# A gated MLP's up projection as seven block products per pair of column blocks, with the hidden values and the residual kept in DRAM and the down projection as a stage of its own

## The chip, the cores and the metric

The kernel runs on one core of one Trainium2 chip. The metric is the device time of one execution in microseconds (us); before the change the median of three runs is 1703.65 us (1700.2 to 1703.98). A core has TensorE (PE; matmuls, and PEld for its weight loads), VectorE (DVE), ScalarE (ACT), GpSimd (POOL) and SyncE (SP). SP issues nearly all DMAs of this kernel, each engine works through its own list in order, and the DMAs themselves run on 16 DMA engines. SBUF is the on-chip memory, PSUM the banks that matmuls write to, DRAM the memory outside the core.

## The reference, cut to what matters

One layer: RMSNorm, an input projection, an attention branch and a state space branch, a gated sum of the two, `w_out` and a residual add, then the channel mixer, which is where the change lies, and a last RMSNorm:

```
xn   = rmsnorm(x, norm2_g)                     # x: 1024 prompt tokens and 8 x 4 sample tokens, 1024 wide
up   = xn @ w_up                               # 1024 x 5632: a value half and a gate half of 2816 columns
val, gate = up[:, :2816], up[:, 2816:]
act  = silu(causal depthwise conv of width 3 over positions of val, + conv_b)
x    = x + (act * gate) @ w_down               # 2816 x 1024
y    = rmsnorm(x, norm_f_g)
```

The last two positions of `val` are outputs too. Everything is float32.

## The kernel before, in words

The 1056 tokens lie along the free axis: four blocks of 264 columns (`C`), each with 256 prompt tokens (every fourth position) and 8 sample tokens, so channels lie on the 128 partitions. A float32 matrix is held as a high and a low part (`split`, L184: an ACT cast, then a DVE subtraction), and a product of two such matrices is three matmuls: low weight by high data, high by low, high by high.

`load_w` (L147 to L157) brings a weight block in by SP (L154), casts its high part on ACT (L155) and subtracts for the low part on DVE (L156), from a pool of two buffers. `gemm` (its matmuls are L174) multiplies 8 blocks of 128 contraction rows in chunks of 352 columns: 8 x 3 x 3 = 72 matmuls for 128 output channels.

The order around the change is this. The merge stage (L1317 to L1330) loads the gated branches back from DRAM (`ck`, 24 loads of 176 KB by SP at L1324, and as many by ACT) and forms the pairs `mh`, `ml`. The `w_out` stage (L1336 to L1355) makes eight blocks `y` = product + residual (`xcol`), which stay in SBUF, their sums of squares on ACT and POOL (L1353, L1354), and the eight pairs `X`. Then, at L1370 to L1381, ones matmuls and transposes give the factors of the norm, `rb2`.

The MLP works on 22 blocks of 128 hidden channels. `up(f)` multiplies the value block, scales it by `rb2` (DVE, L1391), shifts it by one position for the convolution (POOL, L1392 to L1394), forms the convolution (ACT L1396, DVE L1397 and L1398), the silu (ACT L1399) and a product with `rb2` (POOL L1400), then multiplies the gate block and splits the result into `hh`, `hl`. `down` (L1414 to L1419) multiplies a group of three such blocks (the last two groups have two) by `w_down` and adds into `y`; a group's `down` follows the next group's `up`. The last group's `down` is fused with the last norm and the outputs (L1444 to L1510). The convolution states are turned and sent out at L1429 to L1438.

The program is written in this order, and a scheduler orders each engine's list by its own priorities within it; buffers of pools make the waits.

## Time and profile before

| | |
|---|---|
| median of three runs (lowest to highest) | 1703.65 us (1700.2 to 1703.98) |
| the profiled execution's own time; its span | 1697.35 us; 1695.4 us |
| PE, DVE, ACT, POOL busy in the span | 1623.4, 791.0, 490.8, 434.9 us |
| mean granted TensorE clock | 0.984 of full speed |
| DMA over the span | 158.62 MB, 94 GB/s |

The span runs from the first to the last instruction; the profiled execution's time is 1.95 us longer. Each view of the profile counts in us from the span's start. Matmuls are pipelined, so the time that a matmul costs is the distance between the starts of two neighbours and not the duration shown for one.

### The profile page before, as it was taken

To read this page: it belongs to the slowest core of one execution; us is meant where nothing else is said; L and a number is where in the kernel's file an instruction comes from. 1 tells how busy PE (TensorE), PEld (TensorE's weight loads), DVE (VectorE), ACT (ScalarE), POOL (GpSimd) and SP (SyncE) were. 2 spreads that over 40 slices of the span, in tenths; PEclk is the share of its full clock that TensorE was granted. 3 is DMA by queue.
4 is the path that set the end of the run, shared out by engine and by line. 5 is a ranking of instruction groups with operands and counts; after the bars stand their busy time and mean duration, and the time that the engine had idled before them with its cause. 6 is when DMAs were issued, how large, how long until landed. Compare 5 with 4: busy or idle time off the path is not lost.

```text
span 1695.4 us, 25830 instructions
## 1 busy us (share of the span) xinstructions
PE 1623.4 (96%) x10431; PEld 1547.1 (91%) x10431; DVE 791.0 (47%) x1437; ACT 490.8 (29%) x941; POOL 434.9 (26%) x483
## 2 busy tenths in 40 slices
PE   5999978999999989999999999999999999999997
PEld 5898877998888878888999999999999999999996
DVE  5545989233443534235533443434344443444455
ACT  5211221234443433326423222121211212121226
POOL 0669374012122322313322211010111102010115
PEclk9999999999999999999999999999999999999999
DMA  8263311355346445686311110201102021021122
GB/s 228 66 178 120 107 59 51 99 144 134 93 108 149 127 113 195 221 278 189 105 51 38 51 43 24 72 27 50 54 24 72 27 62 43 29 60 33 57 61 103
DMA packets 225010, 158.62 MB, mean 94 GB/s; under 512 B 31173, under 2 KB 210863, under 8 KB 224890
## 3 DMA queue, kind: packets, MB, share of 16 engines
q1 hardware_dynamic: 211210, 135.05, 27.2%
q0 software_dynamic: 3328, 11.54, 2.0%
q10 hardware_dynamic: 10352, 10.38, 1.9%
q8 instruction: 82, 1.34, 0.3%
q14 instruction: 38, 0.31, 0.1%
HBM read 128.97 MB, written 29.92 MB: 94 GB/s over the span
## 4 chain that ended last, share of the span: by engine, by line
PE 55%; DMA 2%; ACT 1%; DVE 1%; POOL 1%; issue 1%; DVEq 0%; ACTq 0%; POOLq 0%; SPq 0%
PE pg L174 53%; DMA msd<-go 1%; PE pa L144 1%; DMA ck<-sgd 1%; DMA go<-sgd 0%; DMA cache<-in_cache_kv_w_dram 0%; PE pD L1225 0%; PE pg L1489 0%; ACT go L1493 0%; PE pg L144 0%; DVE hh L1506 0%; PE pe L144 0%; DVE ml L186 0%; ACT xl L1297 0%; PE pD L1228 0%
## 5 line engine op out<-in xcount | busy, mean ns | idle before, releaser
L174 PE MATMUL pg<-xh,wlo 128*128 128x352 f32 x1872 | 484.2, 332 | 3.0 <-ACT pt__5401 L870 1.5
L174 PE MATMUL pg<-xh,whi 128*128 128x352 f32 x1872 | 470.5, 325 | 0.0
L174 PE MATMUL pg<-xl,whi 128*128 128x352 f32 x1872 | 468.5, 324 | 0.0
L174 PEld LDWEIGHTS pg<-xh,wlo 128*128 128x128 f32 x1872 | 329.5, 189 | 14.5 <-issue 5.6
L174 PEld LDWEIGHTS pg<-xh,whi 128*128 128x128 f32 x1872 | 332.2, 189 | 0.0
L174 PEld LDWEIGHTS pg<-xl,whi 128*128 128x128 f32 x1872 | 331.7, 189 | 0.3
L155 ACT CAST whi<-wraw 128x1024 fp32r<-128x1024 f32 (+2 forms) x154 | 130.9, 850 | 581.4 <-PE pg L174 393.0
L156 DVE TENSOR_TENSOR wlo<-wraw,whi 128x1024 fp32r<-128x1024 f32 (+2 forms) x154 | 162.2, 1053 | 99.5 <-ACT whi L155 96.7
L1392 POOL COPY ext<-ext 128x510 f32<-128x510 f32 x22 | 15.6, 710 | 522.2 <-DVE ext L1391 522.2
L174 PE MATMUL pg<-hh,wlo 128*128 128x352 f32 x480 | 148.0, 325 | 0.0
L174 PE MATMUL pg<-hl,whi 128*128 128x352 f32 x480 | 147.0, 322 | 0.0
L174 PE MATMUL pg<-hh,whi 128*128 128x352 f32 x480 | 146.5, 323 | 0.0
L1419 DVE TENSOR_TENSOR y<-pg,y 128x352 f32<-128x352 f32 x168 | 84.5, 524 | 98.9 <-PE pg L174 98.2
L962 POOL TENSOR_TENSOR qb<-kt,qb 128x512 f32<-128x512 f32 x48 | 64.8, 1364 | 246.3 <-DMA qb<-qd 150.1
L1391 DVE TENSOR_TENSOR ext<-pg,rb 128x352 f32<-128x352 f32 x66 | 32.7, 524 | 154.2 <-PE pg L174 154.2
L174 PEld LDWEIGHTS pg<-hh,wlo 128*128 128x128 f32 x480 | 88.9, 188 | 0.5
L174 PEld LDWEIGHTS pg<-hl,whi 128*128 128x128 f32 x480 | 89.1, 188 | 0.0
L174 PEld LDWEIGHTS pg<-hh,whi 128*128 128x128 f32 x480 | 88.7, 188 | 0.0
L1406 DVE TENSOR_TENSOR go<-pg,cv 128x352 f32<-128x352 f32 x66 | 31.2, 520 | 111.7 <-PE pg L174 111.7
L1400 POOL TENSOR_TENSOR cv<-cv,rb 128x1056 f32<-128x1056 f32 x22 | 54.2, 2463 | 55.0 <-ACT cv L1399 52.7
L1007 ACT COPY pTs<-pT 128x256 f32<-128x256 f32 (+1 forms) x48 | 22.5, 469 | 123.5 <-PE pT L144 121.5
L174 PE MATMUL pg<-yh,wlo 128*128 128x352 f32 x144 | 48.2, 345 | 4.1 <-ACT go L471 3.4
(643 smaller groups left out, 2338.4 us busy)
## 6 DMA issues: line engine op xcount, KB each, us to landing
wraw<-in_w_up_dram SPq DMA_DIRECT2D x44, 512.0 KB
wraw<-in_w_in_dram SPq DMA_DIRECT2D x38, 512.0 KB
qb<-qd SPq DMA_DIRECT2D x48, 256.0 KB
wraw<-in_w_down_dram SPq DMA_DIRECT2D x48, 192.0 KB
sgd<-go SPq DMA_DIRECT2D x16, 528.0 KB
kt<-in_cache_kv_w_dram SPq DMA_DIRECT2D x32, 256.0 KB
cache<-in_cache_kv_w_dram POOLq DMA_DIRECT2D x16, 512.0 KB, 6.5
go<-sgd SPq DMA_DIRECT2D x8, 528.0 KB
```

The costliest lines, as they stand in the source:

```text
L144: PE.transpose(out, in_, ident[:n, :n])
L155: A_.copy(hi, raw)
L156: E2.tensor_tensor(lo, raw, hi.bitcast(F32), OP.subtract)
L174: PE.matmul(ps[c][:, :CH], wt[:, k0 + k, m0:m0 + P], xt[:, c * CH:(c + 1) * CH], start=k == 0 and j == 0, stop=k == n - 1 and j == 2)
L962: G_.tensor_tensor(qb, kv_, qb, OP.mult)
L1007: A_.copy(pTs[:, :2 * n * P], pT[:, :2 * n * P])
L1391: V_.tensor_tensor(ef[:, 2 * C + c * CH:2 * C + (c + 1) * CH], ps[c][:, :CH], rb2[:, cs(c)], OP.mult)
L1392: G_.tensor_copy(e[:, 0:2, 1:256], e[:, 4:6, 0:255])
L1400: G_.tensor_tensor(cv, cv, rb2, OP.mult)
L1406: V_.tensor_tensor(t[:, cs(c)], ps[c][:, :CH], cv[:, cs(c)], OP.mult)
L1419: V_.tensor_tensor(y[m][:, cs(c)], ps[c][:, :CH], y[m][:, cs(c)], OP.add)
```

## The change

`w_up` is used in another way. For each of the 22 hidden blocks the value block V and the gate block G are taken together as one matrix of two block columns, the contraction is cut into two halves of 512 rows, and the tokens into two halves of 528 columns. Seven block products (each 4 x 3 x 2 = 24 matmuls of 264 columns) take the place of eight. The data side needs sums of blocks: `operands` makes seven pairs out of each pair of channel blocks (j, j + 4) with four subtractions and seven splits. The weight side needs four sums and five more splits for each block, and the results are put together by seven additions.

What this moves besides: the residual `xcol` goes to DRAM (`xtd`) and comes back block by block; `y` goes to DRAM (`yd2`), is scaled by the norm's weights in place and is not kept; the gated hidden block goes to DRAM (`hd`). When all 22 blocks are done, `w_down` runs as a stage over four token quarters of 264 columns: each quarter loads its hidden values again, splits them into the places of the operands, loads all of `w_down` (so four times in all), and sends its rows out.

The diff, cut to its core:

```diff
+        xtd = dr.tile([D, T], F32, name="xtd")
+        for k in range(KD):
+            nc.sync.dma_start(xtd[k * P:(k + 1) * P], xcol[k])
...
+        def operands(k, pl, a, b):
+            tA, tB = (yt_.tile([P, T], F32, name="tt", bufs=2) for _ in range(2))
+            V_.tensor_tensor(tA[:, H1], a[:, H2], a[:, H1], OP.subtract)
+            V_.tensor_tensor(tA[:, H2], b[:, H2], tA[:, H1], OP.subtract)
+            V_.tensor_tensor(tB[:, H1], b[:, H2], a[:, H2], OP.subtract)
+            V_.tensor_tensor(tB[:, H2], b[:, H1], tA[:, H2], OP.subtract)
+            XO[k] = {}
+            for o, src in enumerate((a[:, H1], b[:, H1], b[:, H2], tA[:, H1], tA[:, H2], tB[:, H1], tB[:, H2])):
+                hi, lo = (pl.tile([P, HALF], F32R, name=f"x{k}{o}{x}") for x in "hl")
+                split(hi, lo, src)
+                XO[k][o] = (hi, lo)
+        kept = []
+        for j in range(NK):
+            ys = []
+            for m in (j, j + NK):
+                w = load_w(I['w_out'][0][:, m * P:(m + 1) * P], KD, pw=wb)
+                ps = gbanks()
+                gemm(ps, w, list(zip(mh, ml)))
+                y = yt_.tile([P, T], F32, name="yt", bufs=3)
+                nc.sync.dma_start(y, xtd[m * P:(m + 1) * P])
+                for c in range(NCH):
+                    V_.tensor_tensor(y[:, cs(c)], ps[c][:, :CH], y[:, cs(c)], OP.add)
+                nc.sync.dma_start(yd2[m * P:(m + 1) * P], y)
+                if m == 0:
+                    A_.activation(sqa, y, AF.Square)
+                else:
+                    t = yt_.tile([P, T], F32, name="tt", bufs=2)
+                    A_.activation(t, y, AF.Square)
+                    G_.tensor_tensor(sqa, sqa, t, OP.add)
+                A_.activation(y, y, AF.Copy, scale=g2c[:, m:m + 1])
+                ys.append(y)
+            if j < NK - 1:
+                operands(j, xa, *ys)
...
+        operands(NK - 1, xb, *ys)
...
+        def product(w, o):
+            ps = pu_.tile([P, 2, 512], F32, name="pu")
+            for k in range(NK):
+                runs = [(c, j) for j in range(3) for c in range(2)]
+                if k in (0, NK - 1):
+                    runs.sort()
+                for c, j in runs:
+                    wt, xt = ((1, 0), (0, 1), (0, 0))[j]
+                    PE.matmul(ps[:, c, :C], w[wt][:, k], XO[k][o][xt][:, c * C:(c + 1) * C],
+                              start=k == 0 and j == 0, stop=k == NK - 1 and j == 2)
+            return ps[:, :, :C]
...
+            raw = []
+            for c0 in (f * P, DFF + f * P):
+                r = wb.tile([P, KD, P], F32, name="wraw")
+                nc.sync.dma_start(r, I['w_up'][0][:, c0:c0 + P].rearrange("(k p) m -> p k m", p=P))
+                raw.append(r)
+            v, g = raw
+            hi = wb.tile([P, KD, P], F32R, name="whi")
+            lo = wb.tile([P, KD, P], F32R, name="wlo")
+            split(hi, lo, v)
+            A11, A12 = ((hi[:, x:x + NK], lo[:, x:x + NK]) for x in (0, NK))
+            S1, S2, S3, S4_ = (sr.tile([P, NK, P], F32, name=f"S{x}") for x in range(4))
+            V_.tensor_tensor(S1, g[:, :NK], g[:, NK:], OP.add)
+            V_.tensor_tensor(S2, S1, v[:, :NK], OP.subtract)
+            V_.tensor_tensor(S3, v[:, :NK], g[:, :NK], OP.subtract)
+            V_.tensor_tensor(S4_, v[:, NK:], S2, OP.subtract)
+            def parts(src):
+                hi, lo = (sr.tile([P, NK, P], F32R, name=f"s{x}", bufs=6) for x in "hl")
+                split(hi, lo, src)
+                return hi, lo
...
+            s2_, s1_, s3_, s4_, a22 = (parts(t) for t in (S2, S1, S3, S4_, g[:, NK:]))
+            r1, u2, u3, u4 = (h2(ff.tile([P, HALF], F32, name=n)) for n in ("r1", "u2", "u3", "u4"))
+            gt = ff.tile([P, T], F32, name="gt", bufs=2)
+            A_.copy(r1, product(A11, 0))
+            V_.tensor_tensor(u2, product(s2_, 4), r1, OP.add)
+            V_.tensor_tensor(e[:, 2:4], product(A12, 1), r1, OP.add)
+            V_.tensor_tensor(e[:, 2:4], e[:, 2:4], h2(rb2[:, H1]), OP.mult)
+            V_.tensor_tensor(u4, product(s1_, 3), u2, OP.add)
+            m7 = product(s3_, 5)
+            V_.tensor_tensor(h2(gt[:, H2]), m7, u4, OP.add)
+            V_.tensor_tensor(u3, m7, u2, OP.add)
+            V_.tensor_tensor(e[:, 4:6], product(s4_, 2), u4, OP.add)
+            V_.tensor_tensor(e[:, 4:6], e[:, 4:6], h2(rb2[:, H2]), OP.mult)
+            V_.tensor_tensor(h2(gt[:, H1]), product(a22, 6), u3, OP.add)
...
+            V_.tensor_tensor(gt, gt, cv, OP.mult)
+            nc.sync.dma_start(hd[f * P:(f + 1) * P], gt)
+        for f in range(NF):
+            up(f)
...
+            co_ = ff.tile([P, T], F32, name="gt", bufs=2)[:18, :512]
...
+        def hidden(q):
+            out = []
+            for j in range(NH):
+                k, o = places[q % 2 * NH + j]
+                pl = xa if k < NK - 1 else xb
+                hi, lo = (pl.tile([P, HALF], F32R, name=f"x{k}{o}{x}") for x in "hl")
+                r = wb.tile([P, KD, P], F32, name="wraw").rearrange("p k m -> p (k m)")[:, :HALF]
+                nc.sync.dma_start(h2(r), hd[2 * j * P:(2 * j + 2) * P, q * C:(q + 1) * C].rearrange("(f p) c -> p f c", p=P))
+                split(hi, lo, r)
+                out += [(hi[:, x * C:(x + 1) * C], lo[:, x * C:(x + 1) * C]) for x in range(2)]
+            return out
...
+            yo = wb.tile([P, KD, P], F32, name="wlo").rearrange("p k m -> p (k m)")[:rows]
+            A_.activation(yo, yT, AF.Square, accum_out=f[:, 0:1])
+            rsqrt(f[:, 1:2], f[:, 0:1], f[:, 2:3], V_)
+            V_.scalar_tensor_tensor(yo, yT, f[:, 1:2], gf[:rows], OP.mult, OP.mult)
+            nc.sync.dma_start(dst, yo)
...
+        hs_ = hidden(0)
+        for q in range(S4):
+            y = fb.tile([P, KD, C], F32, name="y")
+            nc.sync.dma_start(y, yd2[:, q * C:(q + 1) * C].rearrange("(m p) c -> p m c", p=P))
+            nxt = None
+            yT = [wb.tile([P, KD, P], F32, name="whi").rearrange("p k m -> p (k m)") for _ in range(2)]
+            for m in range(0, KD, 2):
+                ps = [pg.tile([P, 512], F32, name="pd") for _ in range(2)]
+                for k0 in range(0, NF, 4):
+                    n = min(4, NF - k0)
+                    w = load_w(I['w_down'][0][k0 * P:(k0 + n) * P, m * P:(m + 2) * P], n, mw=2 * P, pw=w2,
+                               bufs=({"bufs": 4}, {}))
+                    for x in range(2):
+                        for k in range(n):
+                            xh, xl = hs_[k0 + k]
+                            for j, (wt, xt) in enumerate(((w[1], xh), (w[0], xl), (w[0], xh))):
+                                PE.matmul(ps[x][:, :C], wt[:, k, x * P:(x + 1) * P], xt,
+                                          start=k0 + k == 0 and j == 0, stop=k0 + k == NF - 1 and j == 2)
+                for x in range(2):
+                    V_.tensor_tensor(y[:, m + x], ps[x][:, :C], y[:, m + x], OP.add)
+                if m == 0 and q + 1 < S4:
+                    nxt = hidden(q + 1)
+                if m % 4 == 2:
+                    for b in range(2):
+                        turned_half(yT[b], m // 4, P, lambda k, b=b: y[:, k, b * P:(b + 1) * P])
+            for b in range(2):
+                norm_out(2 * q + b, yT[b], P, ypv[q, b])
+            G_.tensor_copy(sy.rearrange("p k (b s) -> p k b s", s=S4)[:, :, :, q], y[:, :, 256:])
+            hs_ = nxt
```

On SyncE, around the loads for `w_out` (`ck` are the gated branches, `go<-sgd` their first part, `wraw<-in_w_out_dram` a weight block, `xtd<-` a block of the residual on its way to DRAM), before:

```order
L1273 DMA go<-sgd 128x1056 x2
L154 DMA wraw<-in_w_out_dram 128x8x128
L1273 DMA go<-sgd 128x1056
L1281 DMA go<-in_x_sample_dram 32x1024
L1324 DMA ck<-sgd 128x352 x6
L154 DMA wraw<-in_w_out_dram 128x8x128
L1324 DMA ck<-sgd 128x352 x8
L154 DMA wraw<-in_w_out_dram 128x8x128
L1324 DMA ck<-sgd 128x352 x9
L154 DMA wraw<-in_w_out_dram 128x8x128
L1324 DMA ck<-sgd 128x352
L154 DMA wraw<-in_w_out_dram 128x8x128 x4
```

and now:

```order
L1275 DMA go<-sgd 128x1056 x3
L1328 DMA ck<-sgd 128x352 x6
L1283 DMA go<-in_x_sample_dram 32x1024
L1302 DMA xtd<-xl_7610 128x1056 x2
L1302 DMA xtd<-xl_7611 128x1056 x2
L1302 DMA xtd<-xl_7612 128x1056 x2
L1302 DMA xtd<-xl_7613 128x1056 x2
L1328 DMA ck<-sgd 128x352 x18
L156 DMA wraw<-in_w_out_dram 128x8x128
L1372 DMA yt<-xtd 128x1056
L156 DMA wraw<-in_w_out_dram 128x8x128
L1372 DMA yt<-xtd 128x1056 x2
```

The first load for `w_out` stood ahead of all 24 `ck` loads and the next three between them; now it stands behind all 24, and eight writes to `xtd` stand ahead of the last 18.

On SyncE, where the last output of the up projection meets the first weights of the down projection (`out_dram<-` are the convolution states), before:

```order
L1437 DMA out_dram<-go 1x512
L154 DMA wraw<-in_w_down_dram 128x2x128
L1438 DMA out_dram<-go 8x512
L1437 DMA out_dram<-go 1x512
L1438 DMA out_dram<-go 8x512
L1437 DMA out_dram<-go 1x512
L154 DMA wraw<-in_w_down_dram 128x2x128
L1438 DMA out_dram<-go 8x512
L1437 DMA out_dram<-go 1x512
L1438 DMA out_dram<-go 8x512
L1437 DMA out_dram<-go 1x256
```

and now (with what each row waits for, `Activation` being ACT and `DMAHW` an earlier DMA):

```order
L1485 DMA hd<-gt 128x1056 [waits DMAHW4_49,DVE_49]
L1499 DMA out_dram<-gt 8x512 [waits DMAHW5_49]
L1519 DMA wraw<-hd 128x2x264 [waits DMAHW6_49,DMAHW4_49]
L1519 DMA wraw<-hd 128x2x264 [waits DMAHW7_49]
L1498 DMA out_dram<-gt 1x512 [waits DMAHW0_49,Activation_49]
L1499 DMA out_dram<-gt 8x512 [waits DMAHW1_49]
L1498 DMA out_dram<-gt 1x512 [waits DMAHW2_49]
L1499 DMA out_dram<-gt 8x512 [waits DMAHW3_49]
```

and, behind six more of the small outputs:

```order
L1498 DMA out_dram<-gt 1x256 [waits DMAHW2_49]
L1499 DMA out_dram<-gt 8x256 [waits DMAHW3_49]
L1519 DMA wraw<-hd 128x2x264 [waits DMAHW4_49,DVE_49]
L1519 DMA wraw<-hd 128x2x264 [waits DMAHW5_49,DVE_49]
L1547 DMA y<-yd_8218 128x8x264 [waits DMAHW6_49,PE_49]
L156 DMA wraw<-in_w_down_dram 128x4x256 [waits DMAHW0_49,DMAHW1_49,DMASW7_49,DMAHW2_49,DMASW4_49,DMAHW3_49,DMASW3_49,DMAHW7_49,DMASW0_49,Pool_49]
L156 DMA wraw<-in_w_down_dram 128x4x256 [waits DMASW5_49,DMASW1_49]
```

The 24 small outputs lay among weight loads whose products went on. Now all of them stand ahead of the first load of `w_down`, the last twelve behind two loads that wait for the last hidden block's way to DRAM.

On VectorE, one hidden block in the middle of the up projection, before (the block's value half, its gate half and its split; `pg` is PSUM):

```order
L1391 TENSOR_TENSOR ext_8977<-pg,rb_7772 128x352 x3
L156 TENSOR_TENSOR wlo<-wraw,whi 128x1024
L1397 SCALAR_TENSOR_TENSOR cv<-ext_8977,cw,cv 128x1056
L1398 SCALAR_TENSOR_TENSOR cv<-ext_8977,cw,cv 128x1056
L1406 TENSOR_TENSOR go<-pg,cv 128x352 x3
L156 TENSOR_TENSOR wlo<-wraw,whi 128x1024
L186 TENSOR_TENSOR hl<-go,hh 128x1056
```

and now the first half of a block (`S` are sums of weight blocks, `sl` and `wlo` low parts, `pu` PSUM):

```order
L1450 TENSOR_TENSOR S_10569<-wraw 128x512
L1452 TENSOR_TENSOR S_10571<-wraw 128x512
L1451 TENSOR_TENSOR S_10570<-S_10569,wraw 128x512
L1480 SCALAR_TENSOR_TENSOR cv<-ext_9136,cw,cv 128x1056
L1453 TENSOR_TENSOR S_10572<-wraw,S_10570 128x512
L188 TENSOR_TENSOR sl<-S_10570,sh 128x512
L1481 SCALAR_TENSOR_TENSOR cv<-ext_9136,cw,cv 128x1056
L1464 TENSOR_TENSOR u_10361<-pu,r_10360 128x528
L188 TENSOR_TENSOR sl<-S_10569,sh 128x512
L1465 TENSOR_TENSOR ext_9136<-pu,r_10360 128x528
L1466 TENSOR_TENSOR ext_9136<-ext_9136,rb_8208 128x528
L188 TENSOR_TENSOR wlo<-wraw,whi 128x1024
```

The list of a block grew from 11 to 22 instructions, and the first sum of the next block's weights opens it.

## Rows read from the trace of the kernel before

**Rows 1.** The page: engine, busy us, share of the span, instructions.

```profile
PE 1623.4 (96%) x10431; PEld 1547.1 (91%) x10431; DVE 791.0 (47%) x1437; ACT 490.8 (29%) x941; POOL 434.9 (26%) x483
```

**Rows 2.** The chain that ended last, in order of time: start us, us, what.

```profile
761.84 3.94 DMA msd<-go
...
765.91 2.35 DMA go<-in_x_sample_dram
...
807.87 105.01 PE pg L174 x640
...
1265.74 365.68 PE pg L174 x2268
...
1652.59 3.49 PE pg L144 x32
```

**Rows 3.** Timeline of TensorE: start us, us, engine, line, operation; starts are read.

```profile
59.72 0.29 PE L311 MATMUL pg<-xl,uwh 128*128 128x264 f32 x1
...
66.06 0.28 PE L311 MATMUL pg<-xh,uwh 128*128 128x264 f32 x1
...
809.18 0.50 PE L174 MATMUL pg<-ah,whi 128*128 128x352 f32 x1
...
811.23 0.50 PE L174 MATMUL pg<-mh,wlo 128*128 128x352 f32 x1
...
904.32 0.32 PE L174 MATMUL pg<-xh,wlo 128*128 128x352 f32 x1
```

**Rows 4.** Timeline of SyncE, issue of the loads before w_out.

```profile
801.34 0.38 SPq L154 DMA_DIRECT2D wraw<-in_w_out_dram  x1
801.82 12.13 SPq L1324 DMA_DIRECT2D ck<-sgd  x9
...
816.00 0.53 SPq L1324 DMA_DIRECT2D ck<-sgd  x1
```

**Rows 5.** Groups of ScalarE after 900 us: busy us, mean ns, idle before.

```profile
L155 ACT CAST whi<-wraw 128x1024 fp32r<-128x1024 f32 x45 | 47.4, 1054 | 271.2 <-PE pg L174 195.4 <-issue 75.8
L1396 ACT ACTIVATE cv<-ext,cw 128x1056 f32<-128x1056 f32 x22 | 28.0, 1271 | 15.3 <-POOL ext L1392 15.3
...
L1399 ACT ACTIVATE cv<-cv 128x1056 f32<-128x1056 f32 x22 | 23.9, 1087 | 59.3 <-DVE cv L1398 59.3
```

**Rows 6.** Groups of VectorE after 900 us.

```profile
L156 DVE TENSOR_TENSOR wlo<-wraw,whi 128x1024 fp32r<-128x1024 f32 x45 | 55.3, 1229 | 31.3 <-ACT whi L155 31.3
L1391 DVE TENSOR_TENSOR ext<-pg,rb 128x352 f32<-128x352 f32 x66 | 32.7, 524 | 154.2 <-PE pg L174 154.2
...
L1398 DVE SCALAR_TENSOR_TENSOR cv<-ext,cw,cv 128x1056 f32<-128x1056 f32 x22 | 29.3, 1334 | 0.8
...
L156 DVE TENSOR_TENSOR wlo<-wraw,whi 128x384 fp32r<-128x384 f32 x48 | 26.8, 558 | 1.8
...
L1381 DVE COPY rb<-pe 128x512 f32<-128x512 f32 x2 | 1.3, 685 | 0.2 <-PE pe L144 0.2
```

**Rows 7.** Windows: us, busy us and count by engine, clock, DMA share, GB/s.

```profile
660.00:680.00 20.00, 16.60 (x112) 15.71 (x111) 9.64 (x16) 8.81 (x12) 2.02 (x3) 0.91 1.00 368
780.00:790.00 10.00, 9.66 (x61) 8.71 (x60) 3.42 (x7) 5.10 (x15) 3.48 (x4) 0.95 0.20 52
790.00:800.00 10.00, 10.00 (x64) 10.00 (x63) 8.07 (x14) 6.14 (x14) 8.18 (x8) 1.00 0.85 255
```

**Rows 8.** Groups of GpSimd after 900 us.

```profile
L1400 POOL TENSOR_TENSOR cv<-cv,rb 128x1056 f32<-128x1056 f32 x22 | 54.2, 2463 | 55.0 <-ACT cv L1399 52.7 <-issue 2.4
...
L1392 POOL COPY ext<-ext 128x510 f32<-128x510 f32 x22 | 15.6, 710 | 522.2 <-DVE ext L1391 522.2
```

**Rows 9.** Timeline of VectorE and GpSimd, one hidden block.

```profile
1327.91 1.23 DVE L156 TENSOR_TENSOR wlo<-wraw,whi 128x1024 fp32r<-128x1024 f32 x1 [0.60 <-ACT whi L155]
...
1327.99 1.20 POOL L1394 COPY cso<-ext 128x18 f32<-128x18 f32 x1
```

**Rows 10.** Line 1394 on GpSimd, 900 to 1650 us: ns min/median/max, first and last start.

```profile
L1394 POOL COPY cso<-ext x22: 192/1198/1212, 924.1 to 1618.3; 128x18 f32<-128x18 f32 x22
```

188 lines of the change are left out of this document (55 added, 133 removed).

## Prediction

> **What bounds the kernel now.** I read the page first: TensorE is busy 1623.4 of 1695.4 us and VectorE less than half of them [rows 1]. The chain of waits says the same from the other side. From 807.87 us it is one stretch of matmuls after another, the longest 2268 matmuls of 352 columns in 365.68 us, or 0.1612 us each [rows 2]; in the MLP nothing but TensorE sets the time. So the profile pays for fewer matmul columns at that rate, and charges for every wait that gets between two matmuls. The first matmul of the MLP starts at 904.32 us [rows 3], and 791.1 us are left to the end of the span. All sums below set the new length of this part, and what happens ahead of it, against these 791.1 us. They are made against the profiled execution (span 1695.4, own time 1697.35 us), which is 0.4% under the median of the runs, 1703.65; I move the difference over to the median unchanged.
>
> **Matmuls.** Out go 22 x 2 x 72 = 3168 matmuls of the up projection (510.8 us at 0.1612), 1440 of the down projection (232.2 us) and the last group's wide ones. In come 22 x 7 x 24 = 3696 matmuls and 4 x 8 x 22 x 3 = 2112, all of 264 columns. That width is in the trace, with the weights changed at every matmul as here: 52 steps lie between the starts at 59.72 and 66.06 us, 0.1219 us each [rows 3]. The up projection then costs 450.5 us and the down projection 257.5 us. The saving is one product of eight in the up projection alone, and a little of it goes to the narrower matmul: three quarters of 0.1612 would be 0.1209, and at that value the two stages would cost 5.8 us less. I keep 0.1219.
>
> **The start of w_out: 10.5 us later.** Its first weight load stood ahead of the 24 branch loads and was long there. Now it is issued behind the last of them. That one goes out at 816.00 to 816.53 now, and two weight loads with their waits stood ahead of it; without these I take 812.5. The weight load then needs its issue (0.38 [rows 4]), its way (a 528 KB transfer took 3.94 us, a small one 2.35 [rows 2]; I take 3), the ACT cast of 1.05 [rows 5] and the low part, 1.23 [rows 6]: 818.2. Ahead of the last 18 branch loads SP now writes 4.3 MB to DRAM. At 368 GB/s, the most that the trace shows, that is 12 us of all DMA engines, and they are free for 80% of the time from 780 to 790 us and for 15% in the next 10 [rows 7]; I take 2 us of delay, with 0 and 12 as ends. So w_out starts at 820 instead of 811.23 [rows 3], 9 us later, and from idle: between 809.18 and 811.23 a matmul took 0.293 us (7 steps) [rows 3], the pace of the lower clock of 1.2 GHz, which lasted some 12 matmuls after a wait and so costs 1.6 us.
>
> **From w_out into the up projection: 7 us.** Before, the first value block and the gate's weights were ready and the ones matmuls alone waited. Now the last operands are made after the last product. ACT may scale the last y in place only when its copy to DRAM has landed (evacuation 0.5, issue 0.4, way 3, scaling 1.2: about 5 us after w_out's end), and the casts of the weight sums stand behind that scaling on ACT. The first product (2.9 us) needs nothing of it; the second begins about 7 us after the end of w_out, and a later one waits about 1 us for VectorE. I count 5 us of waits and 2 us for the small matmuls that were there before too.
>
> **The up projection: 452.5 us, with 2 us of stalls.** Per block TensorE works 7 x 24 x 0.1219 = 20.5 us. What VectorE must do in that time I price by interpolating: 352 columns from PSUM 0.524 and 512 from PSUM 0.685, so 0.70 for 528; 384 columns in SBUF 0.558 and 1024 in 1.229, so 0.69 for 512 and 0.71 for 528 [rows 6]. Seven additions from PSUM are 4.9, four sums 2.8, five low parts 3.5, the value's low part 1.23, two scalings 1.4, two convolution steps 2.7, the last product 1.25: 17.8 us. To that comes a wait: only two raw buffers exist, so the gate block of the next f is loaded after the last low part of this one is taken, and its first sum stands behind it on VectorE. From that low part to the next one along VectorE's list: load 3.4, then 16.4 us of instructions (17.8 less the two that run in the load's shadow), in all 19.8 us against 20.5. So TensorE stays the bound, by 0.7 us per block. The three PSUM buffers cover single delays of about 3 us. ACT (1.05, five half casts, 1.27, 1.09 and a copy: under 7 us [rows 5]) and POOL (2.46, 0.71 and two tiny copies: under 4 [rows 8]) are far from it. The 2 us of stalls are for the first block; A below has the upper end.
>
> **From up to down: 29 us.** This is the largest charge. Nothing of w_down can be loaded before SP has passed what stands ahead of it. After the last product: the last value rows are scaled, POOL shifts them (0.71 [rows 8]), ACT forms the convolution (1.27) behind one of the six small copies, VectorE adds twice (2.7), ACT takes the silu (1.09 [rows 5]), POOL multiplies (2.46 [rows 8]), VectorE multiplies (1.25); with the handovers the hidden block is issued to DRAM 10 us after the last product and lands at 12.7. SP holds the next reload for that, then issues 12 small outputs, whose copies wait for a shared buffer, two more reloads and 1.1 MB of y, each up to 0.38 us of issue; the first w_down load goes out at about 19.6, lands behind that y at 24.5, and with cast and low part the first matmul runs at 27.4 us. The clock falls in such a wait; 1.6 us as above. As ends I take 18 us (the small outputs find their buffers free) and 38 us (each group of outputs waits its full 3.94 us).
>
> **The down projection: 267.5 us.** Matmuls 257.5; 64 transposes of 0.109 (32 in 3.49 us [rows 2]) are 7.0; stalls 3. Per quarter 64.4 us of matmuls need 11.5 MB of weights, 3.0 of hidden values, 1.1 of y and 1.0 of output: 16.6 MB, 258 GB/s. The trace shows 368 with all DMA engines busy [rows 7], so this fits with a third to spare. The 3 us of stalls are for the first loads of a quarter; the upper end is B.
>
> **The end: 15 us** after the last matmul: an addition and the turns, 1; four copies of half a cast and three squares of a cast on ACT [rows 5], 5.3; two scalings of 1.3 (as L1398 [rows 6]) and a third for the sample rows, 3.9; the factors of the norm between them, 1.5; issue and transfer, 3 (2.35 to 3.94 [rows 2]). The ends are 13 and 19.
>
> Sum: 10.6 + 7 + 452.5 + 29 + 267.5 + 15 = 781.6, against 791.1: 9.5 us less. I round to 9 and forecast **1694.6 us**.
>
> **Rivals.**
> *A. VectorE becomes the bound in the up projection, and the kernel gets slower.* POOL and VectorE hinder one another. At 1327.99 POOL's tiny copy took 1.20 us, ending as VectorE's subtraction from 1327.91 ends [rows 9]; alone it takes 0.19, and half of the 22 take about 1.2 [rows 10]. The other direction matters now: POOL's product of 2.46 us stands beside the scaling and the low parts of the next block, and an instruction that comes 1 us into it and waits for its end loses 1.5 us. A decides from 20.5 - 19.8 = 0.7 us per block. With 1 us lost a block costs 0.3 more, with 2 lost 1.3 more: 7 to 29 us over 22 blocks. I put it at 1.5 lost, 18 us, 1712. The rule for this is in the Trainium skill, "SBUF — State Buffer", Who interferes with whom: VectorE with two SBUF inputs and a GpSimd instruction that reads SBUF exclude each other for whole instructions, and the one that issues later waits. The trace's copy agrees with it (0.19 against 1.20 us), and by it A happens in every block in which the two meet. Against it: the seven additions take only one of their inputs from SBUF, and POOL's product need not fall on a two-input instruction in every block.
> *B. The down stage is bound by its loads.* SP's list mixes weight loads with reloads that wait for two raw buffers, and one wait holds all behind it. If it gets 220 GB/s on average instead of 258, the 66 MB take 300 us and the time is 1735. For it: SP alone issues everything. Against it: three pairs and four raw blocks of weights, each worth 2.9 us of matmuls, are ahead.
> *C. The two transitions cost half.* The outputs' buffers come free earlier, the first weights come at 18 us, and w_out starts only 5 us late: 15 us less, 1680. For it: nearly all of these transfers are small, and 2.35 us is the row for a small one. Against it: w_down's first load stands behind the way of the last hidden block in any case, 12.7 us.
> *D. The transitions cost more.* One of them at its upper end (38 us at the second instead of 27.4) or half of it at both: about 10 more, 1705, no change. For it: each wait there follows the last, so none hides behind another. Against: the ends take every transfer at the slowest row.
>
> **How the numbers follow.** Forecast as above, 1686 to 1702: 0.42. A 0.16, B 0.11, C 0.15, D 0.16. What a measurement of this kernel can tell from no change is about 0.3%, 5 us. Faster by more (below 1698.5): 0.37 of the main case and all of C, 0.52. Within: the other 0.05, 0.13 of D, 0.03 of A, 0.21. Slower: 0.13 of A, all of B, 0.03 of D, 0.27. The range that leaves out two cases in ten runs from 1679 to 1720; it leaves out most of B and the lower half of C.
>
> **What would show it.** Right: 0.122 us per matmul in both stages; TensorE unbroken in the up stage at about 20.5 us per block; a gap of 25 to 30 us before the first matmul of the down stage, ended by the first weights; w_out about 9 us later. Wrong: blocks of more than 21 us with TensorE waiting for VectorE (A); many waits for w_down's casts (B); a gap of under 20 us (C).

## The result

The changed kernel takes 1713.65 us (median of four runs, 1710.27 to 1716.02) beside 1703.2 us for the kernel before: a ratio of 1.0063, 95% interval 1.0042 to 1.0084. It is slower, by about 10 us. The forecast was 1694.6 us, 9 us faster; the time lies inside the range, but the sign was wrong, and the case that was given most weight did not happen.

The profiled execution of the changed kernel has a span of 1714.2 us. The work of TensorE fell as it should; what stands between the stretches of work grew more than that. The page of the changed kernel:

```profile
PE 1576.7 (92%) x11523; PEld 1501.0 (88%) x11523; DVE 1026.5 (60%) x1681; ACT 619.6 (36%) x1113; POOL 406.4 (24%) x419
```

TensorE is busy 46.7 us less than in [rows 1] and yet the span is 18.8 us longer: 65 us more in which it does nothing. TensorE's timeline shows where the largest waits are (start us, us, what, and in brackets the idle time before it and what ended it):

```profile
776.82 1.03 PE L145 MATMUL pa<-ident,go 32*128 32x32 f32 x8 [5.54 <-DMA go<-in_x_sample_dram]
...
831.15 0.66 PE L176 MATMUL pg<-mh,wlo 128*128 128x352 f32 x1 [13.63 <-DVE wlo L158]
...
931.86 0.39 PE L1430 MATMUL pu<-x30l,whi 128*128 128x264 f32 x1 [2.10 <-DVE x30l L188]
...
935.52 0.59 PE L1430 MATMUL pu<-x04h,sl 128*128 128x264 f32 x1 [0.95 <-DVE sl L188]
...
1389.89 0.93 PE L145 MATMUL pe<-ident,cso 128*18 128x128 f32 x7
...
1423.64 0.59 PE L1560 MATMUL pd<-x00h,wlo 128*128 128x264 f32 x1 [16.80 <-DVE wlo L158]
```

The reader is to see two gaps. One stands ahead of `w_out`: the residual's transposes wait 5.54 us for x_sample (1.44 before), and `w_out`'s first matmul starts from idle at 831.15, where [rows 3] has it at 811.23. The other lies between the last matmul of the up projection (just ahead of 1389.89) and the first of the down projection at 1423.64, 33.75 us with only a few small transposes in it.

Against that stand the two stages themselves. The chain of waits has 208 us of the up projection in one piece:

```profile
1162.06 208.32 PE pu L1430 x1710
```

That is 0.1218 us for each matmul, as was forecast from [rows 3]. Term by term, the sum against the 1685.9 us of span that the forecast amounts to (904.32 + 781.6):

| term | forecast | measured | more |
|---|---|---|---|
| start of w_out | 820 | 831.15 | 11.2 |
| w_out itself, from cold | 94.9 | 95.3 | 0.4 |
| w_out's end to the end of up | 459.5 | 463.5 | 4.0 |
| last up matmul to first down matmul | 27.4 | 33.75 | 6.4 |
| down, with its cold start | 269.1 | 273.1 | 4.0 |
| end | 15 | 17.5 | 2.5 |

Every row errs to the same side: 28.5 us in all, of which the first and the fourth are 17.6. The forecast column stands on the one profiled execution of the kernel before.

The profiled executions don't stand for the medians in equal measure. That of before is 6 us under the median of its runs, that of after 2 us over its own, so the two spans differ by 18.8 us and the medians by 10.5. A second profile of the kernel before (e15, below) is 7.9 us longer than the first, 5.6 of them ahead of `w_out`; measured by it, 5.6 us of the first row of the table are not the change.

### The profile page after: what moved, and what is told of

It reads as the page before. It is cut to its first block, busy times and chain, and to the rows that moved or that the text cites. A ratio compares the mean times of both kernels' runs of the same rounds, so it can differ in the third digit from the quotient of the medians.

```text
span 1714.2 us, 28810 instructions
## 1 busy us (share of the span) xinstructions
PE 1576.7 (92%) x11523; PEld 1501.0 (88%) x11523; DVE 1026.5 (60%) x1681; ACT 619.6 (36%) x1113; POOL 406.4 (24%) x419
## 5 line engine op out<-in xcount | busy, mean ns | idle before, releaser
L158 DVE TENSOR_TENSOR wlo<-wraw,whi 128x1024 fp32r<-128x1024 f32 (+1 forms) x148 | 182.7, 1235 | 166.2 <-ACT whi L157 160.5
L176 PE MATMUL pg<-xh,wlo 128*128 128x352 f32 x816 | 213.5, 343 | 4.1 <-ACT pt__5401 L872 2.7
L157 ACT CAST whi<-wraw 128x1024 fp32r<-128x1024 f32 (+1 forms) x148 | 148.2, 1003 | 173.6 <-PE pd L1560 114.9
L176 PE MATMUL pg<-xh,whi 128*128 128x352 f32 x816 | 199.8, 326 | 0.0
L176 PE MATMUL pg<-xl,whi 128*128 128x352 f32 x816 | 199.0, 325 | 0.0
L176 PEld LDWEIGHTS pg<-xh,wlo 128*128 128x128 f32 x816 | 142.4, 191 | 15.2 <-issue 5.6
L176 PEld LDWEIGHTS pg<-xh,whi 128*128 128x128 f32 x816 | 144.7, 190 | 0.0
L176 PEld LDWEIGHTS pg<-xl,whi 128*128 128x128 f32 x816 | 144.4, 191 | 0.3
L187 ACT CAST sh<-S 128x512 fp32r<-128x512 f32 x88 | 52.2, 619 | 77.8 <-DVE S L1451 57.1
L188 DVE TENSOR_TENSOR sl<-S,sh 128x512 fp32r<-128x512 f32 x88 | 61.8, 704 | 0.5 <-ACT sh L187 0.5
L1466 DVE TENSOR_TENSOR ext<-ext,rb 128x528 f32<-128x528 f32 x22 | 48.5, 2204 | 0.7
```

Of the source, the lines that this page charges most:

```text
L157: A_.copy(hi, raw)
L158: E2.tensor_tensor(lo, raw, hi.bitcast(F32), OP.subtract)
L176: PE.matmul(ps[c][:, :CH], wt[:, k0 + k, m0:m0 + P], xt[:, c * CH:(c + 1) * CH], start=k == 0 and j == 0, stop=k == n - 1 and j == 2)
L187: A_.copy(hi, src)
L188: V_.tensor_tensor(lo, src, hi.bitcast(F32), OP.subtract)
L1466: V_.tensor_tensor(e[:, 2:4], e[:, 2:4], h2(rb2[:, H1]), OP.mult)
```

## The experiments

Ratios are those to the kernel before, measured anew beside each group of experiments (medians of 1699.2 to 1701.9 us), with 95% intervals. Where two changed kernels are compared, the difference is taken from their ratios. "The changed kernel" is the one of the result. The first six, with a second profile of the kernel before among them, are on the start of `w_out`.

**e1, the weights of w_out early.** The first two blocks of `w_out` are loaded through the old buffers, the first (issued at 760.60) ahead of all 24 `ck` loads, the second (775.45) behind six of them.

```diff
+        w_first = {m: load_w(I['w_out'][0][:, m * P:(m + 1) * P], KD) for m in (0, KD // 2)}
         s6a.close()
...
-                w = load_w(I['w_out'][0][:, m * P:(m + 1) * P], KD, pw=wb)
+                w = w_first[m] if m in w_first else load_w(I['w_out'][0][:, m * P:(m + 1) * P], KD, pw=wb)
```

> The first two weight blocks of w_out are loaded into the old weight buffers, so that they need not stand behind the 24 branch loads. Theory (place in SyncE's list): TensorE was idle 13.6 us before w_out's first matmul at 831.15 us; it starts the first product about 13 us earlier and ends it with the last branch block (ready at 829.5), so all that follows comes 11 to 14 us earlier: about 1701. Rival (the branch blocks themselves are late, because the writes of the residual fill the DMA engines): the first product waits for them, only load, cast and low part of the first weights go, 3 us: about 1710.

1701.49 us, ratio 1.0006 (0.9991 to 1.0021): 10 us less than the changed kernel. Behind the wait for x_sample, 5.17 us here, TensorE's only wait ahead of `w_out` is now

```profile
805.72 0.66 PE L176 MATMUL pg<-ah,wlo 128*128 128x352 f32 x1 [3.77 <-DVE ck L1332]
```

and `w_out` ends at 911.3 instead of 926.6. With its weights there, `w_out`'s first product runs while the merge stage is still at work, and the wait of 13.63 us is gone. To move two weight loads is enough to bring the kernel level with the one before.

**e2, the residual's writes off SyncE's list.** The eight writes to `xtd` are issued by GpSimd.

```diff
-            nc.sync.dma_start(xtd[k * P:(k + 1) * P], xcol[k])
+            nc.gpsimd.dma_start(xtd[k * P:(k + 1) * P], xcol[k])
```

> The eight writes of the residual to DRAM are issued by GpSimd instead of SyncE, all else the same. Theory (SyncE's list): the last 18 branch loads were held from 788.3 to 797.1 us by these writes; they start 8 us earlier, and w_out too: about 1706. Rival (the DMA engines): the 4.3 MB take the same 12 us of the engines wherever they are issued, the branch loads land no earlier, 0 to 2 us: about 1713.

1712.05 us, ratio 1.0070 (1.0042 to 1.0098); `w_out` starts at 833.27. No gain: from the merge's first matmul to `w_out`'s it is 41.2 us (792.09 to 833.27) where the changed kernel has 41.5, so it is not the 8.8 us of SyncE's list that cost.

**e10, one write instead of eight.** Here the residual is that of one block for all eight, so the traffic of seven writes is gone and the reads stay.

```diff
-        for k in range(KD):
-            nc.sync.dma_start(xtd[k * P:(k + 1) * P], xcol[k])
+        nc.sync.dma_start(xtd[0:P], xcol[0])
...
-                nc.sync.dma_start(y, xtd[m * P:(m + 1) * P])
+                nc.sync.dma_start(y, xtd[0:P])
```

> The changed kernel with one of the eight residual blocks written to DRAM and read back eight times, so seven writes of 540 KB are left out and the residual added is wrong. Theory (the writes take the DMA engines from the branch loads, wherever they are issued): the last 18 branch loads start and land 7 to 9 us earlier, and w_out starts at 822 to 824 instead of 831 us: 1705. Rival (the branch loads' pace is set by GpSimd and VectorE, and w_out's start by its weights alone): under 3 us, 1711 or more.

1707.71 us, ratio 1.0038 (1.0020 to 1.0055), 4 us less; `w_out` starts at 826.35, 4.8 us earlier, of which 0.9 lie ahead of the merge's first matmul (788.78 instead of 789.67). So seven of the writes cost about 4 us. With e2 this points to the DMA engines: from 790 to 800 us they are busy all the time in the changed kernel (share 1.02) and about half of it in e10 (0.54), and the last 18 `ck` loads take 25.5 us of SyncE's list there and 23.8 in e10. SyncE's timeline of the changed kernel (start, us, what):

```profile
765.98 4.96 SPq L1328 DMA_DIRECT2D ck<-sgd  x6
772.57 0.34 SPq L1283 DMA_DIRECT2D go<-in_x_sample_dram  x1
788.26 8.76 SPq L1302 DMA_DIRECT2D xtd<-xl  x8
797.12 25.49 SPq L1328 DMA_DIRECT2D ck<-sgd  x18
822.70 0.39 SPq L156 DMA_DIRECT2D wraw<-in_w_out_dram  x1
```

**e11, x_sample issued by GpSimd.** In that timeline six `ck` loads stand ahead of x_sample; before, x_sample was issued first, at 765.91. This swap stood in the order rows ahead of the prediction, and the sum gave it nothing. What it costs is the question of e11, e13 and e15.

```diff
-        nc.sync.dma_start(xsr, I['x_sample'].rearrange("b t d -> (b t) d"))
+        nc.gpsimd.dma_start(xsr, I['x_sample'].rearrange("b t d -> (b t) d"))
```

> The changed kernel with the load of x_sample (L1283) issued by GpSimd, so that it no longer stands behind the six transfers of L1328 on SyncE's list; nothing else moved. Theory (the load's place behind those six is what delays the residual transposes and with them the attention products by about 6 us): the load lands some 5 us earlier, w_out's matmuls start near 825 instead of 831, and the time is 1708 (1706 to 1710). Rival 1 (the load waits for its buffer, or GpSimd reaches it as late, so the place on the list is not what holds it): w_out starts within 2 us of 831 and the time is 1713 to 1715. Rival 2 (the transposes come earlier, but w_out's weights arrive behind the same transfers of L1328 at the end, so the start is set by the DMA engines): the transposes near 770, the start still 829 to 831, the time 1712 to 1714.

1714.68 us, ratio 1.0079 (1.0050 to 1.0107): no change, and the transposes wait as long as before:

```profile
775.59 1.03 PE L145 MATMUL pa<-ident,go 32*128 32x32 f32 x8 [6.14 <-DMA go<-in_x_sample_dram]
```

The load now goes out from GpSimd's list, where it waited until 770.95 us. The experiment did not take away what held it: x_sample lands in a `go` buffer, which comes free only when an earlier gated branch has reached DRAM, and that write is issued among the six `ck` loads: from its issue at 765.07 the load waited 5.9 us, where [rows 2] has 3.94 for the same write. That the `ck` loads are what delays it is argued from these rows and was not tried by itself.

**e13, x_sample early in a buffer of its own.**

```diff
+        xsr = pool("xs", 1, stack=s5_).tile([32, D], F32, name="xs")
+        nc.sync.dma_start(xsr, I['x_sample'].rearrange("b t d -> (b t) d"))
         for m in range(KD):
...
-        xsr = go.tile([P, T], F32, name="go")[:32, :D]
-        nc.sync.dma_start(xsr, I['x_sample'].rearrange("b t d -> (b t) d"))
```

> The changed kernel with x_sample loaded into a buffer of its own some hundred us earlier, so that neither its place on a list nor the buffer that it waited for holds it. Theory (the late x_sample is what holds the residual's transposes and with them the attention products: 5.5 us of idle TensorE ahead of the transposes in the changed kernel, 1.4 before): no wait for x_sample, w_out starts near 826 (5 earlier), time 1709 (1707 to 1711). Rival (the start of w_out is set by the 18 loads of L1328 and the weights behind them, so what is gained ahead of them is lost again): w_out starts within 1.5 us of 831 and the time is 1713 to 1715.

1705.96 us, ratio 1.0026 (1.0011 to 1.0041): 6 us less than the changed kernel. TensorE's timeline has no wait for x_sample any more, and

```profile
773.51 0.66 PE L145 MATMUL pa<-ident,xh 128*128 128x128 f32 x4 [1.97 <-ACT xl L1299]
...
823.73 0.66 PE L176 MATMUL pg<-mh,wlo 128*128 128x352 f32 x1 [13.58 <-DVE wlo L158]
```

`w_out` starts 7.4 us earlier, behind the same wait for its weights. About 2 of the 7.4 lie in the execution (the last gated branch goes to DRAM at 771.59 here and at 773.68 in the changed kernel), the other 5 are x_sample. So everything ahead of `w_out` moved as one, which the rival of e13 had denied. That says what an early x_sample gains, not what the change lost by it: the kernel before waits for x_sample too.

**e15, the kernel before, once more.** Nothing is edited.

> The kernel before, unchanged, for a second profile of it: how much of the 19.9 us by which w_out starts later lies in the one execution that the sum was made against (its own time 1697.35 is 6 us under the median of its runs). Theory (all of it is the change): w_out starts within 1 us of 811.2. Rival (the profiled execution was a short one ahead of w_out): it starts 3 to 6 us later, and the time is 1701 to 1704.

1700.8 us, ratio 1.0002 (0.9987 to 1.0016). The new profile has a span of 1703.3 us, 7.9 more than the first, and

```profile
774.82 0.65 PE L144 MATMUL pa<-ident,go 32*128 32x32 f32 x8 [1.53 <-DMA go<-in_x_sample_dram]
...
816.88 0.50 PE L174 MATMUL pg<-mh,wlo 128*128 128x352 f32 x1
```

`w_out` starts at 816.88, 5.6 us later than in [rows 3]; the last gated branch goes out at 773.93 instead of 767.61. From `w_out`'s start to the end the two executions take 884.2 and 886.4 us. So the first profile was a short one ahead of `w_out`. (This one was the longest of its ten executions, 4.5 us over their median, so 5.6 is the distance between a short and a long one.)

Where the change lost the other 14.3 us is read from the first matmul of the merge, in the changed kernel and in e15:

```profile
789.67 0.41 PE L176 MATMUL pg<-ah,wlo 128*128 128x352 f32 x1
```

```profile
789.57 0.41 PE L174 MATMUL pg<-ah,wlo 128*128 128x352 f32 x1
```

Against e15 nothing is lost ahead of it, x_sample included: TensorE waits for x_sample 4 us longer in the changed kernel (5.54 against 1.53), but it came to that wait 2 us earlier, and its transposes then run without waits and take 1.9 us less. Against the first profile (783.69) the loss is 6.0, which e15 has without the change. From the merge's first matmul to `w_out`'s first it is 27.5 and 27.3 us in the two profiles of the kernel before and 41.5 in the changed one: 14 us, and all of it lies here. The merge does not end later. Its last low part is made at the same time in e15 and, with what follows it, in the changed kernel:

```profile
829.05 0.53 DVE L186 TENSOR_TENSOR ml<-ck,mh 128x352 fp32r<-128x352 f32 x1 [1.36 <-ACT mh L185]
```

```profile
828.92 0.53 DVE L188 TENSOR_TENSOR ml<-ck,mh 128x352 fp32r<-128x352 f32 x1 [0.17 <-ACT mh L187]
829.87 1.23 DVE L158 TENSOR_TENSOR wlo<-wraw,whi 128x1024 fp32r<-128x1024 f32 x1 [0.42 <-ACT whi L157]
```

In the kernel before, `w_out` runs for 12 us by then, on weights that came long ago; in the changed kernel the first weights are only now cast. So the 14 us are the place of the weight load, which e1 showed from the other side. The 4 us of the writes (e10) are a part of them: in e10 too the weights follow the merge's last pair, which is ready earlier.

Three experiments are on the gap between up and down.

**e3, two raw buffers for w_down.**

```diff
-                               bufs=({"bufs": 4}, {}))
+                               bufs=({"bufs": 2}, {}))
```

> Two raw buffers for w_down instead of four, so that the pool fits where the weight sums lay; the first two loads of w_down then stand ahead of the small outputs in SyncE's list. Theory (memory that is freed late, and SyncE's list behind it, make the gap of 33.7 us between the last matmul of the up projection and the first of the down projection): the gap falls to 5 to 10 us. With two buffers the loads of the down stage are at the edge (load 3.4, cast 1.05, low part 1.23 for two blocks of 2.93 us of matmuls) and may give back 5 to 15 us: 1695 to 1708. Rival (the gap is the way of the last hidden block to DRAM and back): it stays above 25 us, 1710 or more.

1735.42 us, ratio 1.0202 (1.0167 to 1.0236). The gap falls to 6.6 us and the stage behind it starves. TensorE's timeline and, of the down stage, its windows (us, busy us and count of PE, PEld, DVE, ACT and POOL, clock, DMA share, GB/s):

```profile
1394.81 0.59 PE L1560 MATMUL pd<-x00h,wlo 128*128 128x264 f32 x1 [2.97 <-DVE wlo L158]
```

```profile
1400.00:1500.00 100.00, 80.78 (x627) 77.98 (x626) 50.26 (x70) 45.97 (x63) 0.30 (x1) 0.95 0.73 234
...
1600.00:1700.00 100.00, 91.23 (x733) 89.31 (x733) 43.87 (x58) 36.41 (x44) 0.30 (x1) 1.00 0.52 170
```

The first weights of `w_down` now come while the up projection still runs. The order of SyncE's list says why: in the changed kernel their first load waits for GpSimd and for nine DMAs, here the first for TensorE and four of GpSimd's DMAs and the second for TensorE alone, because the larger pool reaches into memory that the last hidden block uses and the smaller one does not:

```
L156 DMA wraw<-in_w_down_dram 128x4x256 [waits DMASW5_49,DMASW2_49,DMASW6_49,DMASW1_49,PE_49]
L156 DMA wraw<-in_w_down_dram 128x4x256 [waits PE_49]
L1498 DMA out_dram<-gt 1x512 [waits Activation_49]
```

The addresses of the built kernels say the same. Within a partition, the weight sums and their parts lie in bytes 167008 to 199776. The changed kernel's ten buffers for `w_down`, of 4096 bytes each, end there too and begin at 158816, in `gt` and `cv`; `gt` holds the last hidden block and then the small outputs. With eight buffers the pool begins at 167008. So the first weights wait for the last hidden block's way because they take its memory, not because they need the block (e5 and e9, whose pools also begin at 167008, lose the gap too). But two raw buffers feed only 81 to 91 us of matmuls in 100, and the stage takes 45 us longer than the changed kernel's. This is rival B's mechanism, come about in another way.

**e5, the same memory taken from the cast parts** (with e1's edit): two high and two low buffers instead of three, four raw ones as before.

```diff
-        w2 = pool("w2", 3, stack=s9, side="right")
+        w2 = pool("w2", 2, stack=s9, side="right")
```

> As the first experiment (first two blocks of w_out early, 1701.5 us), and in the down stage two buffers for high and low parts instead of three, with four raw buffers kept: the pool then lies where the weight sums lay, and the first loads of w_down go ahead of the small outputs. Theory (the gap of 33.7 us between up and down is memory freed late with SyncE's list behind it, and the third experiment lost its gain to two raw buffers in the down stage): gap 5 to 8 us, down stage within 10 us of 273: 1675 to 1688. Rival (the down stage needs every buffer): it starves as in the third experiment, 1700 to 1715.

1705.01 us, ratio 1.0026 (1.0005 to 1.0047), 3 us more than e1. The gap is 7 us, and the down stage takes 301 us with about 21 us of waits behind the gap for the low parts of `w_down`. The explanation then was that at the joint of two column pairs a group of two blocks is only 1.46 us of matmuls, less than the cast and low part of the next (1.05 + 1.24), and that with two pairs of buffers nothing is ahead; e8 tries it.

**e6, no convolution states** (with e1's edit): they are neither turned nor written.

```diff
-        for f0 in range(0, NF, 4):
-            n = min(4, NF - f0)
...
-                nc.sync.dma_start(O[13][0, :, i, f0 * P:(f0 + n) * P], co_[9 * i + 1:9 * i + 9, :n * P])
```

> As the first experiment, and the convolution states are neither turned nor written out (this leaves out two of the small outputs). The first load of w_down then stands right behind the reload of the last hidden block and the load of y. Theory (the gap is a chain: last hidden block 15.6 us, small outputs 5.5, reloads and y 1.8, first weights 8.3, cast and low part 2.4): only the small outputs' 5 to 6 us go, the gap is 27 to 29 us: 1695. Rival (the small outputs' buffers hold the last hidden block as well): gap under 20 us, 1687 or less.

1689.18 us, ratio 0.9932 (0.9910 to 0.9954), 13 us less than e1. In TensorE's timeline the gap is one wait:

```profile
1400.03 0.56 PE L1551 MATMUL pd<-x00h,wlo 128*128 128x264 f32 x1 [25.17 <-DVE wlo L158]
```

About 9 of e1's 34 us were the small outputs. The chain of waits of the changed kernel has the other 25 (start us, us, what):

```profile
1392.49 1.18 ACT cv L1479
1393.69 1.33 DVE cv L1480
...
1396.40 1.09 ACT cv L1482
...
1397.62 2.42 POOL cv L1483
1400.07 1.27 DVE gt L1484
1401.35 4.09 DMA hd<-gt
...
1407.40 2.01 DMA out_dram<-gt
...
1412.92 8.34 DMA wraw<-in_w_down_dram
1421.29 1.05 ACT whi L157
1422.36 1.24 DVE wlo L158
...
1423.64 5.66 PE pd L1560 x24
```

Two experiments are on VectorE in the up projection.

**e4, one more sum per block on VectorE.** The fourth sum is computed twice, which adds 0.6 us to a block.

```diff
             V_.tensor_tensor(S4_, v[:, NK:], S2, OP.subtract)
+            V_.tensor_tensor(S4_, v[:, NK:], S2, OP.subtract)
```

> The fourth weight sum is computed twice, so VectorE has one more instruction of 0.68 us (0.6 us from start to start) in each of the 22 blocks of the up projection; nothing else changes. Theory (VectorE's list is at its own end in a block, 20.5 us, as TensorE's matmuls are): every block takes 0.6 us more, 13 us in all: about 1727. Rival (TensorE alone sets the block and VectorE has 1 us or more to spare): no change, 1714.

1726.68 us, ratio 1.0146 (1.0114 to 1.0178), 14 us more than the changed kernel. In the profile the up stage is 6.8 us longer (0.31 per block) and `w_out` starts 3.6 us later, which the edit doesn't touch. So half of an added 0.6 us shows: VectorE's list has some 0.3 us per block to spare, no more.

**e7, the product with rb2 on VectorE** (with e1's edit). GpSimd's long product is gone, and VectorE has 1.25 us more of its own.

```diff
-            G_.tensor_tensor(cv, cv, rb2, OP.mult)
+            V_.tensor_tensor(cv, cv, rb2, OP.mult)
```

> As the first experiment, and the product of the activation with the norm's factor, 22 of 2.47 us, moves from GpSimd to VectorE (about 1.2 us each there). Theory (that product holds VectorE's scaling up to 2.44 us instead of 0.70; TensorE and VectorE each need 20.5 us per block): VectorE's list gets 0.5 us shorter per block, TensorE's matmuls still set the block: no change or up to 3 us, 1699 to 1701. Rival A of the prediction in full (VectorE alone sets the block): 0.5 x 22 = 11 us less, 1690.

1695.21 us, ratio 0.9963 (0.9946 to 0.9980), 7 us less than e1; the up stage takes 458.9 us instead of 462.9. In the groups of VectorE (busy us, mean ns) the scaling that was struck is the first row for the changed kernel:

```profile
L1466 DVE TENSOR_TENSOR ext<-ext,rb 128x528 f32<-128x528 f32 x22 | 48.5, 2204 | 0.7
L1472 DVE TENSOR_TENSOR ext<-ext,rb 128x528 f32<-128x528 f32 x22 | 15.3, 696 | 0.0
```

and in e7, a line further down in the file:

```profile
L1467 DVE TENSOR_TENSOR ext<-ext,rb 128x528 f32<-128x528 f32 x22 | 15.4, 701 | 0.0
```

More work on VectorE made the kernel faster: the 1.5 us that it had lost to GpSimd in each block were more than the 1.25 that it took on.

The last experiments put the parts together, on e7: **e8** with groups of 4, 4, 4, 4, 3, 3 blocks of `w_down` and two pairs of cast buffers, **e9** with groups of two, six raw buffers and five pairs, each half as large, **e12** as e9 with e11's edit, and **e14** as e9 with e13's.

```diff
-        w2 = pool("w2", 3, stack=s9, side="right")
+        w2 = pool("w2", 5, stack=s9, side="right")
...
-                for k0 in range(0, NF, 4):
-                    n = min(4, NF - k0)
+                for k0, n in zip([0, 2, 4, 6, 8, 10, 12, 14, 16, 18, 20], [2, 2, 2, 2, 2, 2, 2, 2, 2, 2, 2]):
...
-                               bufs=({"bufs": 4}, {}))
+                               bufs=({"bufs": 6}, {}), kd=4)
```

> w_out's first blocks early, the norm factor's product on VectorE (1695.2 us together), two high and low buffers in the down stage as in the fifth experiment, and w_down in groups of 4, 4, 4, 4, 3, 3 hidden blocks instead of 4, 4, 4, 4, 4, 2. Theory (with two such buffers cast and low part, 2.5 us with the handovers, must fit beside the matmuls of one group; a group of two is 1.46 us and TensorE waits 0.7 us at each of the 16 joints, one of three is 2.2 us): gap between up and down 6 us instead of 33, 0.7 us per joint go, 1668 to 1680. Rival (reloads of hidden values ahead in the engines' lists make the waits): the down stage still takes over 290 us, 1690.

1692.7 us, ratio 0.9951 (0.9936 to 0.9966). The gap is 6.8 us, but the down stage still takes 294.8 us with about 14 us of waits for low parts behind the gap, so the group of two blocks was the smaller part of what e5 lost.

> The same, but w_down in eleven groups of two hidden blocks (256 KB), six raw buffers and five high and low ones in the same memory. Theory: finer pieces are five groups of 1.46 us deep, so waits of up to 5 us are covered: 1665 to 1675, and below the eighth experiment. Rival (a small load pays its fixed parts more often: 176 loads instead of 96, each 0.4 us of SyncE's list): above the eighth.

1675.73 us, ratio 0.9859 (0.9832 to 0.9886). The gap is 4.9 us and the down stage 280.1.

> The kernel with the first two w_out blocks loaded early, the recombination product of L1483 on VectorE, groups of two blocks of w_down with six raw and five cast buffers, and the load of x_sample issued by GpSimd. Theory (x_sample's place delays the start of w_out by 6 us, and with the weights in place nothing else holds the start): 1670 (1667 to 1673), against 1675.7 without the last edit. Rival (the place of that load is not on the path, or the order of the other products holds the start): 1674 to 1677, with w_out starting where it started without the last edit.

1674.94 us, ratio 0.9860 (0.9824 to 0.9896): as in e11, nothing.

> The kernel with the first two w_out blocks loaded early, the product of L1483 on VectorE and groups of two blocks of w_down, and x_sample loaded early into a buffer of its own. Theory (here w_out's weights are in place, so the 5 us of the transposes come through in full): 1670 (1667 to 1673). Rival (the loads of L1328 set the start of w_out): 1674 to 1677.

1671.46 us, ratio 0.9827 (0.9804 to 0.9849), the fastest of all; against e9 5 us. In its timeline `w_out` starts without a wait, and the gap is two short ones:

```profile
813.96 0.43 PE L176 MATMUL pg<-mh,wlo 128*128 128x352 f32 x1
...
1367.90 0.60 PE L145 MATMUL pe<-ident,cso 128*18 128x128 f32 x4 [1.17 <-ACT gt L1497]
1370.94 0.39 PE L1560 MATMUL pd<-x00h,wlo 128*128 128x264 f32 x1 [2.44 <-DVE wlo L158]
```

Against the changed kernel's profile (span 1666.3, 47.9 less), `w_out` ends 19.4 us earlier, up takes 4.6 less, the gap is 4.9 instead of about 34, and the down stage takes 278.1 instead of 273.1, since its groups are smaller and the DMAs more.

## Why the prediction was wrong

The forecast failed at the stretches between the stages of matmuls, which it priced too low: by 5.3 us ahead of `w_out` (taken against e15) and by 6.4 from up to down, with 11 us in smaller terms. The change was to give 9 us and took 10.

- **The matmuls: right.** 0.1218 us per matmul in the up projection against 0.1219, and TensorE unbroken there, busy for 219.49 of the 220 us from 1160 on (columns as in e3's windows). The seventh product instead of the eighth is worth what it was said to be.

```profile
1160.00:1380.00 220.00, 219.49 (x1804) 219.09 (x1804) 189.63 (x238) 74.31 (x98) 42.08 (x44) 1.00 0.25 80
```

- **The start of w_out: the step that failed first, right in kind and too short.** The working followed the first load of `w_out` along SyncE's list, and that load's place is what cost (e1, e15). It gave the writes 2 us where seven of them took about 4 (e10). And it let the cast and the low part follow the load at once, 5.7 us from issue to matmul; it was 8.45 (822.70 to 831.15), because ACT has the cast behind the merge's last one, which waited for GpSimd:

```profile
828.41 0.48 ACT L187 CAST mh<-ck 128x352 fp32r<-128x352 f32 x1 [0.68 <-POOL ck L1333]
828.80 1.04 ACT L157 CAST whi<-wraw 128x1024 fp32r<-128x1024 f32 x1
```

  To that come 5.6 us that are not the change at all but the execution that the sum was made against. Taken with e15's start, 816.88 + 9 = 825.9 was forecast and 831.15 measured. That x_sample had changed places with six `ck` loads was not seen at all; against e15 it did not show in the start of the merge, and what it costs in other executions is open.
- **From up to down: right in kind, low by 6.4.** Each station of the working can be found in the chain. The hidden block goes out 11.5 us after the last product (10 in the working), lands at 15.6 (12.7), the first load of `w_down` goes out at 23.0 (19.6). The larger miss is its way: 8.34 us, where the working had 4.9 (19.6 to 24.5); four such loads and a 1.1 MB block go out together there. What the working did not see is that this chain need not be one: the first weights waited for memory (e3, e9), and what looked like a fixed cost of 27 us can be had for 5.
- **Rival A: its mechanism in nearly every block, its price wrong.** The scaling at L1466 takes 2204 ns on average (about 2440 in 19 of the 22 blocks) where the same instruction at L1472 takes 696, so 1.5 us are lost per block, just the value put on it. TensorE lost about 4 us by it (e7), not 18. VectorE's timeline of the changed kernel, with GpSimd's below it, shows the margin:

```profile
1217.33 0.69 DVE L1465 TENSOR_TENSOR ext<-pu,r 128x528 f32<-128x528 f32 x1
1218.06 2.44 DVE L1466 TENSOR_TENSOR ext<-ext,rb 128x528 f32<-128x528 f32 x1
1220.43 1.22 DVE L188 TENSOR_TENSOR wlo<-wraw,whi 128x1024 fp32r<-128x1024 f32 x1
...
1222.73 0.69 DVE L1467 TENSOR_TENSOR u<-pu,u 128x528 f32<-128x528 f32 x1
1223.35 0.68 DVE L188 TENSOR_TENSOR sl<-S,sh 128x512 fp32r<-128x512 f32 x1
...
1231.14 0.69 DVE L1450 TENSOR_TENSOR S<-wraw 128x512 f32<-128x512 f32 x1 [2.84 <-DMA wraw<-in_w_up_dram]
...
1238.57 2.45 DVE L1466 TENSOR_TENSOR ext<-ext,rb 128x528 f32<-128x528 f32 x1
```

```profile
1217.46 2.48 POOL L1483 TENSOR_TENSOR cv<-cv,rb 128x1056 f32<-128x1056 f32 x1 [3.04 <-ACT cv L1482]
```

  The scaling's end, 1220.50, is some 0.5 us behind that of GpSimd's product, 1219.94. The two instructions from 1222.73 are shown as 0.69 and 0.68 us long, but start 0.62 apart: they overlap. The working added durations, 17.8 us for a block. With the loss in it, VectorE is busy for 189.63 of the 220 us from 1160, or 17.7 us per block: the overlap, about 10%, covered the loss. The wait of 2.84 us for the next gate block is the one that the working had priced at 3.4. VectorE's round is 20.51 us (1218.06 to 1238.57), as long as TensorE's; as each waits for the other, that alone does not say which of them sets it. e4 and e7 do: of 0.6 us more for VectorE half shows, and 0.25 less gives back 0.2, so the two are nearly level.
- **Rivals B and C: not so.** The down stage got its weights: waits of 0.7 to 1.8 us at three joints, 4 us in all, at 249 GB/s between 1500 and 1600 us. The miss of 4 is 1 in these waits, 1 in the cold start, and most of the rest a second stretch at a lower clock behind the last of them (0.84 from 1580 to 1590 us). **D** is nearest to what came: both transitions cost more than forecast. It was put at 10 us more, 1705; the medians say 19 more, 1713.65, and the table 28.5, with the difference between executions in it. It had a chance of 0.16 because its ends had been read as the slowest of each step; but apart from the 2 us for the writes, no step of it counted what other transfers do to the one that is waited for.
- **Small terms.** The entry into the up projection and the stage itself took 4 us more than allowed, about as much as e7 gave back; the end 2.5 more.

## What to carry to other kernels

Saving work on the engine that bounds pays only if the order of the loads ahead of each stage is kept: go through every row that changed place on the DMA queue, and ask of a load that moves back which work now waits behind it (14 us here, for one weight block). Small loads count too: 128 KB brought early gained about 6 us (e13), though no change had been meant there. When a stage begins with an idle gap, look at what its first load waits for; if that is a buffer's memory and not data, a smaller or differently cut pool removes the gap (34 us to 5 here), as long as it still feeds the stage. And profile the kernel before a second time ahead of a sum against one execution: here the two differed by 5.6 us at the very place that was disputed.
